# Splitting projection weights on ScalarE and VectorE, and weighting the token's own share of the shift while reading PSUM

## The chip, the cores and the metric

The kernel runs on one core of a Trainium2 chip. The metric is the device time of one execution in microseconds. The kernel before takes 4546.02 us (median of 3 runs, 4545.11 to 4547.92). The engines are named as in the profile: PE (TensorE matmul), PEld (its weight loads), DVE (VectorE), ACT (ScalarE), POOL (GpSimd), SP (the queue that issues most DMAs).

## The reference, cut to what matters

Two layers of a hybrid trunk over 2048 latent tokens and 256 context tokens, width 1024. Each layer normalises, projects into 32 blocks of 128 columns, mixes in three head groups, and projects back. The change touches only the input projection and the shift over tokens that follows it for the RWKV columns:

```python
def centred_shift(p, mu_prev, mu_next):
    prev = jnp.pad(p, ((0, 0), (1, 0), (0, 0)))[:, :-1]
    nxt = jnp.pad(p, ((0, 0), (0, 1), (0, 0)))[:, 1:]
    return p + mu_prev * (prev - p) + mu_next * (nxt - p)

    h = rms_norm(x, norm_w[l]) * (1.0 + scale) + shift
    ...
    pa, pb, pt = _split(h @ w_in[l], (RWKV_COLS, HGRN_COLS, ATTN_COLS))
    ...
    pa = centred_shift(pa.astype(F32), mu_prev, mu_next)
    r, k, v, wd_f, wd_b, ad_f, ad_b, g = _split(pa, RWKV_SPLITS)
```

The first 14 of the 32 blocks (`pa`) are shifted. The kernel computes the shift as (1 - mu_prev - mu_next) p + mu_prev prev + mu_next next; the first of these three weights is `mu0` in its code.

## The kernel before, in words

**Stages.** Each layer has an input projection (`inproj_phase`) and then a mixing phase (`phase2`: the RWKV and HGRN recurrences, the attention, the readout and the output projection). In the profile the input projection of the first layer runs from the start to about 1190 us, that of the second from about 2310 to 3495 us; the mixing phases fill the rest.

**The projection.** Activations lie in SBUF with features on partitions and tokens along the free dimension, as a rounded part and a remainder (`hi`, `lo`). The weights of one 128-column block arrive as 128 x 1024 float32 (`wraw`, one buffer, loaded from the POOL queue, L304) and are split in the same way by `split` (L307): `whi` is the rounded copy (L312) and `wlo` the remainder (the tensor_tensor of L313, which the trace records at the helper's line, L74). Each of the two has two buffers, so the split of block n+1 waits until PE is through with block n-1. `prefetch(n+1)` splits the next block and starts the load of the one after it; that load waits until the split has read `wraw`. A product is 24 matmuls into a PSUM tile `ps` (three buffers): whi and wlo against h's rounded part, and whi against its remainder.

**Two sweeps.** The tokens are done in two sweeps: 1280 tokens (as groups of 512, 256 and 512), then 1024 (two groups of 512). In each sweep the blocks follow one another in the list `order`: 32 in the first layer and 33 in the second, so there are 130 splits in all.

**After a group** (`group`, L339). ACT copies `ps` into `s` (two buffers) for unshifted blocks, and into `pb` (one buffer, with a column more on each side) for shifted ones. In the second layer the blocks in `free` leave out the context tokens.

**After a block** (`end`, L379). For a shifted block, DVE makes `s` from `pb`, for each segment of tokens: a tensor_scalar with mu0 (L392, recorded as L79) and two scalar_tensor_tensor that add the two neighbours (L393 and L394, recorded as L83). Then `post` runs what the block needs and stores it. After it, `behind` lets the preparation of the RWKV recurrence (`RwkvPrep`) advance: from the block at position 9 on, its matmuls (tiles `aps`, `apm`), its DVE work (`tk`, `th`, `lkk`, and the row-by-row inverses `Gs` and `inv`, 60 dependent instructions for one window) and its round trips to memory (`scr_Lx`, `scr_Dx`, `daT`) lie between the projection's matmuls on the same engines.

**Order.** Every engine executes its instructions strictly in the order of its own stream. That order is made at build time by a planner that simulates the engines, puts an instruction in when its inputs are ready in that simulation, and prefers what the program wrote earlier. At run time each instruction waits for its semaphores, and what stands behind it on its engine waits with it.

Beside the splits, POOL does the remainders of the activations for three quarters of each normalised block (`h`, L74), the edges of `pb` (L373, L375, L376, L385), and the load of `wraw`.

Of the kernel before, what the change touches and what calls it, by code (L numbers as in the profile page):

```python
# [9 lines left out]
F32 = mybir.dt.float32  # L10
# [3 lines left out]
AF = mybir.ActivationFunctionType  # L14
ALU = mybir.AluOpType
# [27 lines left out]
def W(ap, n):  # L43
    return ap[:, n:n + 1]


class Trunk:
# [227 lines left out]
    def inproj_phase(self, l, src, prep, start):  # L275
        nc, io, S = self.nc, self.io, self.scr
# [6 lines left out]
        with ExitStack() as ph:  # L283
# [23 lines left out]
            def split(n):  # L307
                if n < len(seq):
                    w = raw.pop(n)
                    hi = wsp.tile([128, KD, 128], F32R, name="whi", tag="whi")  # L310
                    lo = wsp.tile([128, KD, 128], F32R, name="wlo", tag="wlo")
                    nc.gpsimd.tensor_copy(hi, w)  # L312
                    self.tt(lo, w, hi.bitcast(F32), ALU.subtract, nc.gpsimd)  # L313
                    spl[n] = (hi, lo)

            def prefetch(n):
                if n in raw:
                    split(n)
                    load(n + 1)
# [19 lines left out]
            def group(sw, n, st, t0, bn, every):  # L339

                j, s, pb, skip, shifted = st
                hi, lo = spl[n]
                base = 1280 * sw
                c0, c1 = BLK if skip and t0 == 0 else 0, BLK + 2 if shifted and t0 == 0 else BLK
                if c0 >= c1:
                    return
                ps = self.pin.tile([128, 512], F32, name="ps", tag="ps")
                if bn > BLK:
                    c1 = bn
                hh, hl = h[t0]  # L350
                i = 0
                for k, wt, ht in [(k, wt, hh) for k in range(KD) for wt in (hi, lo)] + [(k, hi, hl) for k in range(KD)]:
                    self.mm(ps[:, c0:c1], wt[:, k, :], ht[:, k, c0:c1], i == 0, i == 23)
                    i += 1
                    if i % every == 0 and work:
                        next(work[0], None)
                if not shifted:
                    self.evac(l, j, s[:, t0 - base:t0 - base + bn], ps[:, 0:bn], t0 - base, bn)
                else:
                    o = t0 - base + (1 if t0 == 0 or sw else 2)  # L360
                    if c0 == 0:
                        self.act(pb[:, o:o + bn], ps[:, 0:bn], AF.Identity)
                    if t0 == 0:
                        self.act(pb[:, 1282:1283], ps[:, BLK:BLK + 1], AF.Identity)

# [13 lines left out]
            def end(sw, n, st):  # L379
                j, s, pb, skip, shifted = st  # L380
                spl.pop(n, None)
                base = 1280 * sw
                if shifted:
                    if sw == 0:
                        edge.tensor_copy(keep[:, j], pb[:, 1281:1282])  # L385
                        segs = [(256, 1024, 258)] + ([] if skip else [(0, 256, 1)])
                    else:
                        segs = [(1280, 1024, 1)]
                    m0, mp, mn = W(self.mu0[l], j), W(self.P(l, "mup"), j), W(self.P(l, "mun"), j)
                    for t0, bn, c in segs:  # L390
                        sv = s[:, t0 - base:t0 - base + bn]
                        self.ts(sv, pb[:, c:c + bn], m0, ALU.mult)  # L392
                        self.stt(sv, pb[:, c - 1:c - 1 + bn], mp, sv, ALU.mult, ALU.add)  # L393
                        self.stt(sv, pb[:, c + 1:c + 1 + bn], mn, sv, ALU.mult, ALU.add)  # L394
                blks = sorted(SWEEP[sw])
                if skip:
                    blks = [b for b in blks if b[0] > 0]
                self.post(l, j, s, base, blks)
# [19 lines left out]
            for sw in range(2):  # L418
                for pos in [0] + list(range(2, end_ + 1)):
                    n = len(order) * sw + pos  # L420
                    pair = range(2 if pos in (0, end_) else 1)
                    prefetch(n + 1)
                    sts = [begin(sw, order[pos + e]) for e in pair]
                    for gi, g in enumerate(SWEEP[sw]):
                        while any(a not in done for a in cut(g)):
                            next(work[0], None)
                        for e in pair:
                            group(sw, n + e, sts[e], g[0], g[1], 4 if n == 0 and gi == 0 else 6)
                            if g is SWEEP[sw][-1]:
                                if len(pair) == 2 and e == 0:  # L430
                                    spl.pop(n)
                                    prefetch(n + 2)
                                end(sw, n + e, sts[e])
                                behind(sw, pos + e)
                        if sw == 0 and pos == end_ and gi == 0:

                            work[0] = norm(cuts[1][:2], cuts[1][2:])
                    if sw == 0 and pos == end_:
                        while cuts[1][1] not in done:
                            next(work[0], None)  # L440
                        for _ in work[0]:
                            pass
                        work[0] = norm(cuts[1][2:])
                    if sw == 0 and pos == end_ - 2:
                        for a in cuts[1][:2]:
                            xn[a] = self.normed(l, src, a, BLK)
# [1204 lines left out]
```

## Time and profile before

| | |
|---|---|
| median of 3 runs | 4546.02 us |
| the profiled execution | 4540.61 us, its span 4538.8 us |
| granted clock of PE over the span | 0.929 of full speed |
| PE busy | 3941.3 us (87%) |
| DVE busy | 3164.2 us (70%) |
| ACT busy | 1984.9 us (44%) |
| POOL busy | 1390.9 us (31%) |
| POOL, rounded weights, 130 casts | 151.6 us |
| POOL, weight remainders, 130 subtractions | 335.3 us |
| DVE, own share of the shift, 78 products | 62.1 us |

Busy time is time in which an engine executes; issuing of DMAs and waiting for semaphores is not in it. The clock of PE has two levels, 2.4 GHz (1.0 in the profile) and 1.2 GHz (0.5); a mean of 0.92 over a stretch says that 16% of it ran at the lower one. Where a line of the trace has "idle before", it is the time in which the engine had nothing to execute just before, and the name behind the arrow is what ended it.

### The profile page before, as it was taken

Reading aid. Unit: us, or ns where it says so; the run is one execution under the profiler, and the core shown is the slowest. Engines: PE = TensorE matmul, PEld = TensorE weight load, DVE = VectorE, ACT = ScalarE, POOL = GpSimd, SP = SyncE. Lnnn points to the kernel's source line nnn. Section 1 sums busy time; section 2 is a strip of 40 time slices with the busy share of each in tenths; the row PEclk is TensorE's granted clock in tenths of the full one; section 3 lists DMA queues with packets and bytes.
Section 4 is the critical chain, followed back from the end, with each engine's and each line's share of the span. In section 5 each row is a group of like instructions: output and inputs, shape, how many; then the busy total and the mean of one; then the engine's idle time right before and its main releaser. Section 6 shows DMA issues by size and latency. Waiting matters only on the chain. (4 is left out here: it accounts for less than half of the span.)

```text
span 4538.8 us, 98552 instructions
## 1 busy us (share of the span) xinstructions
PE 3941.3 (87%) x39424; PEld 3217.7 (71%) x39424; DVE 3164.2 (70%) x5646; ACT 1984.9 (44%) x4050; POOL 1390.9 (31%) x1298
## 2 busy tenths in 40 slices
PE   7998898889789889868979988898887888988788
PEld 4767776777677777766758767776676777777676
DVE  3547777678577887777744777556775877777786
ACT  3414343443355555533424353333433555555443
POOL 2322233223233332242243212243222422333232
PEclk8999898999899999988989989899898999999899
DMA  5466654666643334346634476435665543334554
GB/s 202 144 200 197 198 158 121 190 197 190 167 123 107 106 105 115 91 118 214 209 117 129 143 231 195 116 106 172 197 185 159 135 113 101 97 104 126 171 187 132
DMA packets 777312, 688.41 MB, mean 152 GB/s; under 512 B 352164, under 2 KB 675044, under 8 KB 776856
## 3 DMA queue, kind: packets, MB, share of 16 engines
q1 hardware_dynamic: 747624, 583.93, 43.4%
q0 software_dynamic: 18720, 68.17, 5.2%
q10 hardware_dynamic: 10512, 30.02, 2.0%
q8 instruction: 312, 5.11, 0.5%
q14 instruction: 144, 1.18, 0.1%
HBM read 440.70 MB, written 241.22 MB: 150 GB/s over the span
## 5 line engine op out<-in xcount | busy, mean ns | idle before, releaser
L67 PE MATMUL ps<-h,whi 128*128 128x512 f32 x4160 | 1374.7, 406 | 18.2 <-ACT s L64 11.2
L67 PEld LDWEIGHTS ps<-h,whi 128*128 128x128 f32 x4160 | 806.0, 195 | 207.7 <-issue 19.5
L67 PE MATMUL ps<-h,wlo 128*128 128x512 f32 x2080 | 850.9, 409 | 5.2 <-POOL wlo L74 5.2
L312 POOL CAST whi<-wraw 128x1024 fp32r<-128x1024 f32 x130 | 151.6, 1166 | 1124.0 <-PE ps L67 991.8
L67 PEld LDWEIGHTS ps<-h,wlo 128*128 128x128 f32 x2080 | 411.7, 198 | 95.4 <-POOL wlo L74 6.3
L74 POOL TENSOR_TENSOR hE<-hb 128x256 f32<-128x256 f32 x408 | 290.9, 735 | 326.7 <-PE wps L67 195.7
L74 POOL TENSOR_TENSOR wlo<-wraw,whi 128x1024 fp32r<-128x1024 f32 x130 | 335.3, 2579 | 10.5
L1085 DVE COPY_PREDICATED hatt<-lm,wps 64x256 f32<-64x256 int32 x476 | 266.7, 560 | 29.8 <-PE wps L67 23.2
L64 ACT ACT_TABLE_LOAD x177 | 227.1, 1283 | 109.9 <-DVE s L79 33.4
L74 DVE TENSOR_TENSOR Gs<-can,inv 128x30 f32<-128x30 f32 (+9 forms) x540 | 238.9, 442 | 35.0 <-PE apm L67 23.7
L67 PE MATMUL pq<-KZ,BKs 128*64 128x128 f32 x2496 | 228.2, 297 | 34.9 <-DMA KZ<-scr_RK 18.8
L67 PE MATMUL opo<-wohi,ohi 128*128 128x512 f32 x544 | 216.2, 413 | 31.2 <-DVE og L74 18.6
L74 DVE TENSOR_TENSOR hQz<-hE,hqz 128x512 f32<-128x512 f32 x204 | 179.8, 882 | 76.4 <-DMA hqz<-scr_hq 67.8
L74 DVE TENSOR_TENSOR inv<-inv,Gs 128x30 f32<-128x30 f32 (+9 forms) x540 | 223.5, 414 | 12.1
L83 DVE SCALAR_TENSOR_TENSOR s<-pb,par,s 128x1024 f32<-128x1024 f32 (+1 forms) x156 | 217.3, 1393 | 5.6
L67 PE MATMUL opo<-wolo,ohi 128*128 128x512 f32 x544 | 212.9, 407 | 0.0
L64 ACT ACTIVATE pt<-wps 128x512 f32<-128x512 f32 (+1 forms) x288 | 149.4, 525 | 137.1 <-PE wps L71 132.7
L67 PEld LDWEIGHTS pq<-KZ,BKs 128*64 128x64 f32 x2496 | 169.4, 147 | 53.6 <-issue 19.8
L64 ACT ACTIVATE s<-ps 128x512 f32<-128x512 f32 (+1 forms) x175 | 95.8, 562 | 251.6 <-PE ps L67 222.8
L64 ACT ACTIVATE pb<-ps 128x512 f32<-128x512 f32 (+2 forms) x162 | 77.1, 492 | 290.5 <-PE ps L67 204.1
L71 PE MATMUL wps<-ident,prob 128*128 128x128 f32 x960 | 168.7, 292 | 40.8 <-DVE hatt L1085 22.8
L79 DVE TENSOR_SCALAR s<-pb,mu 128x1024 f32<-128x1024 f32 (+1 forms) x78 | 62.1, 796 | 194.7 <-ACT pb L64 193.9
(272 smaller groups left out, 9225.8 us busy)
## 6 DMA issues: line engine op xcount, KB each, us to landing
wraw<-in_w_in_dram POOLq DMA_DIRECT2D x128, 512.0 KB, 4.6
scr_KB<-tk SPq DMA_DIRECT2D x36, 768.0 KB
BKs<-scr_KB SPq DMA_DIRECT2D x144, 192.0 KB
KZ<-scr_RK SPq DMA_DIRECT2D x272, 96.0 KB
x<-in_mod_w_dram SPq DMA_DIRECT2D x32, 512.0 KB
lkk<-scr_kk SPq DMA_DIRECT2D x36, 384.0 KB
th<-scr_wa SPq DMA_DIRECT2D x36, 384.0 KB
scr_RK<-lkk SPq DMA_DIRECT2D x36, 384.0 KB
```

The source lines that it names most:

```text
L64: return self.nc.scalar.activation(out=out, in_=in_, func=func, **kw)
L67: return self.nc.tensor.matmul(out=out, lhsT=lhsT, rhs=rhs, start=start, stop=stop)
L71: return self.nc.tensor.transpose(out, in_, self.ident[0:p, 0:p])
L74: return (eng or self.nc.vector).tensor_tensor(out=out, in0=a, in1=b, op=op)
L79: return e.tensor_scalar(out=out, in0=a, scalar1=s1, scalar2=None, op0=op0)
L83: return (eng or self.nc.vector).scalar_tensor_tensor(out=out, in0=a, scalar=s, in1=b, op0=op0, op1=op1)
L312: nc.gpsimd.tensor_copy(hi, w)
L1085: nc.vector.copy_predicated(o, m, d)
```

## The change

`split` makes the rounded copy with an ACT activation (Identity) and the remainder with a DVE tensor_tensor, where POOL did both. In `group`, ACT reads each shifted product a second time from PSUM and writes it, multiplied by mu0, to `s`; in `end` DVE's multiplication by mu0 is gone, and its two additions stay.

```diff
@@ split
-                    nc.gpsimd.tensor_copy(hi, w)
-                    self.tt(lo, w, hi.bitcast(F32), ALU.subtract, nc.gpsimd)
+                    self.act(hi, w, AF.Identity)
+                    self.tt(lo, w, hi.bitcast(F32), ALU.subtract)
@@ group
                     if c0 == 0:
                         self.act(pb[:, o:o + bn], ps[:, 0:bn], AF.Identity)
+                        self.act(s[:, t0 - base:t0 - base + bn], ps[:, 0:bn], AF.Identity, scale=W(self.mu0[l], j))
@@ end
-                    m0, mp, mn = W(self.mu0[l], j), W(self.P(l, "mup"), j), W(self.P(l, "mun"), j)
+                    mp, mn = W(self.P(l, "mup"), j), W(self.P(l, "mun"), j)
                     for t0, bn, c in segs:
                         sv = s[:, t0 - base:t0 - base + bn]
-                        self.ts(sv, pb[:, c:c + bn], m0, ALU.mult)
                         self.stt(sv, pb[:, c - 1:c - 1 + bn], mp, sv, ALU.mult, ALU.add)
```

## Rows read from the trace of the kernel before

**Rows 1.** Stretches of the input projections: engines' busy us (instructions), clock, DMA share, GB/s.
```profile
60.00:350.00 290.00, 282.60 (x1369) 207.15 (x1368) 136.98 (x176) 102.50 (x164) 82.15 (x79) 0.98 0.54 169
350.00:1190.00 840.00, 741.62 (x5466) 613.60 (x5464) 625.72 (x1118) 343.10 (x545) 245.70 (x197) 0.92 0.59 177
2390.00:2550.00 160.00, 154.79 (x805) 130.15 (x803) 82.23 (x96) 65.19 (x101) 47.19 (x47) 0.95 0.41 124
2550.00:3495.00 945.00, 819.98 (x5855) 662.25 (x5854) 642.12 (x1144) 367.53 (x571) 265.13 (x217) 0.91 0.56 167
```
**Rows 2.** PE's waits, 350 to 1190 us: total us, times, longest us.
```profile
PE apm L67 <- DMA daT<-scr_Dx: 25.3, 13, 4.2
PE aps L67 <- DVE tk L699: 15.6, 7, 4.0
PE aps L67 <- DVE tk L74: 15.4, 6, 5.1
PE ps L67 <- POOL wlo L74: 2.0, 1, 2.0
```
**Rows 3.** PE's waits, 2550 to 3495 us.
```profile
PE apm L67 <- DMA daT<-scr_Dx: 37.7, 21, 8.1
PE aps L67 <- DVE tk L74: 18.5, 5, 9.8
PE ps L67 <- ACT s L64: 11.2, 3, 7.3
PE aps L67 <- DVE tk L699: 10.0, 6, 2.2
```
**Rows 4.** Costliest groups: busy us, mean ns | idle before, releasers.
```profile
L312 POOL CAST whi<-wraw 128x1024 fp32r<-128x1024 f32 x130 | 151.6, 1166 | 1124.0 <-PE ps L67 991.8
L74 POOL TENSOR_TENSOR wlo<-wraw,whi 128x1024 fp32r<-128x1024 f32 x130 | 335.3, 2579 | 10.5
L79 DVE TENSOR_SCALAR s<-pb,mu 128x1024 f32<-128x1024 f32 (+1 forms) x78 | 62.1, 796 | 194.7 <-ACT pb L64 193.9
```
**Rows 5.** POOL's timeline at 494 us: start us, us, instruction.
```profile
494.19 2.40 POOL L74 TENSOR_TENSOR wlo<-wraw,whi 128x1024 fp32r<-128x1024 f32 x1
```
**Rows 6.** DVE's timeline at 494 us.
```profile
494.34 2.47 DVE L74 TENSOR_TENSOR Gs<-can,inv 128x198 f32<-128x198 f32 x1
496.84 0.37 DVE L74 TENSOR_TENSOR inv<-inv,Gs 128x198 f32<-128x198 f32 x1
```
**Rows 7.** DVE's timeline, first and last instruction of the count.
```profile
115.82 3.09 DVE L83 SCALAR_TENSOR_TENSOR s<-pb,par,s 128x256 f32<-128x256 f32 x2
...
3459.08 2.42 DVE L74 TENSOR_TENSOR Gs<-can,inv 128x150 f32<-128x150 f32 x1
```
**Rows 8.** PE's timeline: first, one and last wait of the count.
```profile
146.37 1.13 PE L67 MATMUL pa<-t,bones 128*128 128x512 f32 x2 [0.32 <-ACT t L64]
...
504.61 1.65 PE L67 MATMUL aps<-lkk,tk 64*64 64x64 f32 x26 [5.06 <-DVE tk L74]
...
3373.26 2.04 PE L67 MATMUL aps<-lkk,tk 64*64 64x64 f32 x47 [4.32 <-DVE tk L74]
```
**Rows 9.** DVE, one group by shape: busy us, mean ns | idle before.
```profile
L83 DVE SCALAR_TENSOR_TENSOR s<-pb,par,s 128x1024 f32<-128x1024 f32 x112 | 193.2, 1725 | 4.5
```
**Rows 10.** Tile `s`: duration ns min/median/max, first and last start us, forms.
```profile
L83 DVE SCALAR_TENSOR_TENSOR s<-pb,par,s x156: 457/1277/3417, 115.8 to 3429.3; 128x1024 f32<-128x1024 f32 x112, 128x256 f32<-128x256 f32 x44
```
**Rows 11.** Tile `pb`: duration ns min/median/max, first and last start us, forms.
```profile
L74 DVE TENSOR_TENSOR s<-s,pb x8: 1224/1357/1493, 326.1 to 973.4; 128x1280 f32<-128x1280 f32 x4, 128x1024 f32<-128x1024 f32 x4
```
**Rows 12.** ACT groups by shape: busy us, mean ns | idle before, releasers.
```profile
L64 ACT ACTIVATE s<-ps 128x512 f32<-128x512 f32 x148 | 86.8, 595 | 224.3 <-PE ps L67 195.5 <-DMA scr_aq<-s 12.3 <-DMA scr_sgr<-s 8.1
L64 ACT ACTIVATE th<-aps,half 128x256 f32<-128x256 f32 x108 | 43.3, 472 | 85.3 <-PE aps L67 78.9 <-DVE Gs L74 5.3 <-DMA scr_Dx<-can 0.8
L64 ACT ACTIVATE t<-s,par 128x512 f32<-128x512 f32 x24 | 17.1, 713 | 42.5 <-DVE s L83 42.5
L64 ACT ACTIVATE wohi<-wo 128x1024 fp32r<-128x1024 f32 x16 | 16.8, 1052 | 21.1 <-DMA wo<-in_w_out_dram 21.0
```

## The prediction

> **What bounds the kernel now.** The change lies in the two input projections, so I read them first, by stretch (from 60 and 2390 us on, when the projection's matmuls run). In the 2235 us of [rows 1] PE is busy 283 + 742 + 155 + 820 = 1999 us: it is the engine that sets the end, and it idles 236 us. Its clock adds a second loss: the granted 0.98, 0.92, 0.95 and 0.91 leave 6 + 67 + 8 + 85 = 166 us of full speed unused, so each idle microsecond goes with 0.70 us lost at the lower level. DVE is busy 1487 us there (67%), ACT 878 us (39%). Nearly all of the loss is in the stretches from 350 and 2550 us, in which the RWKV preparation shares the engines; the two before them idle 13 us.
>
> Then PE's waits in those two stretches [rows 2, 3]. It waits for DVE's `tk` (L699 and L74: 59.5 us) and for `daT` (63 us), whose round trip starts when DVE and ACT are through with an inverse. It waits for a split only 2.0 us in the first stretch. So POOL's 487 us of splitting [rows 4] are hidden as far as their own completion goes, and making them shorter is worth nothing by itself.
>
> The third view is the timelines of POOL and DVE beside each other, and it shows what the splits do cost. At 494.19 POOL starts a remainder and takes 2.40 us [rows 5]; at 494.34 DVE starts a product of 128x198, which lasts 2.47 us, and the next instruction, of the same shape, 0.37 us [rows 6]. The two end together. DVE was held until POOL was done, and ten microseconds later PE waits 5.06 us for DVE's `tk` [rows 8]. After 60 us I counted 106 DVE instructions of the projections that overlap a split and run over 1 us longer than the 20th percentile of their own kind; [rows 7] has the first and the last of them. Their excess is 211 us; with the smaller ones it is 267 us. The lowest estimate that rows give alone: the 112 long additions of the shift average 1725 ns [rows 9] where the median of all is 1277 [rows 10], 112 x 0.448 = 50 us in this one group.
>
> The Trainium skill has a rule for this (SBUF — State Buffer, "Who interferes with whom"): VectorE and GpSimd share one pair of ports, a VectorE instruction with two SBUF inputs contends with a GpSimd instruction that reads SBUF, and the second one is blocked until the first is through. The 494 us rows agree. If every one of the 130 remainders blocked DVE for its whole mean, the held time would be 335 us and the forecast below would come out near 4467 us by the same steps; the counted 211 us decide.
>
> **The change part by part.**
>
> *Taken from DVE.* The 78 products with mu0, 62 us [rows 4], and the held time, of which I take 211 us (ends 50 and 267). Together 273 us.
>
> *Added to DVE.* 130 subtractions of 128x1024 with two SBUF inputs. The nearest rows are the 128x1024 and 128x1280 subtractions and minima on `s`, 1224 ns at least and 1493 at most [rows 11]: 130 x 1.224 = 159 us, which I take because the minimum is that of the 1024 shape; 194 us at the other end. So DVE's net relief is 273 - 159 = 114 us, 0.42 of what goes (0.29 with 194 us added, 0.52 with 267 us held; with 50 us held it would be a loss of 47 us).
>
> *What PE gains from it.* Of 117 waits of PE over 0.3 us in these stretches, 58 come within 8 us after a DVE instruction that was held by over 1 us in all ([rows 8]: the first, one, and the last). Each can shrink at most by the held time before it: 85 us in all, as the upper limit of what the removal alone could give. Since the subtractions return part of the load to DVE's stream, I take the same 0.42 of it: 36 us (25 to 44). With 0.70 us of clock for each of them, 25 us more (0 to 31).
>
> *Added to ACT.* 130 casts at 1.052 us, the same shape and conversion as `wohi` [rows 12]: 137 us. 112 scaled reads of 512 and 22 of 256 columns. No row has this form: an unscaled read of 512 takes 0.595 us, an activation of 512 with a scale from a parameter tile 0.713, one of 256 with a bias tile 0.472 [rows 12]. I take 0.65 and 0.47, 83 us (75 to 90). ACT goes from 878 to about 1098 us, 49% of the stretches. Three PSUM buffers of 24 matmuls each cover a late read; PE waited 11.2 us for ACT's `s` in the second projection [rows 3], and a quarter more load makes that 3 us more.
>
> *Moved earlier: the claim on `s`.* A shifted block now writes `s` at its first group, not after its last. The buffer must be free of block n-2: its DVE work and its stores. If it isn't, ACT stands, and behind it the reads of later groups and the preparation's exponentials. Today's 148 unshifted reads lose 12.3 + 8.1 us of ACT's time to such stores [rows 12]; as much for 112 more is 15 us, and PE sees a third, 5 us. With the 3 us above, ACT's side costs 8 us (0 to 20).
>
> *New waits.* The rounded copy waits for the last matmul of block n-1, as it does on POOL, which stood there 992 us in all [rows 4]. On ACT the read of that same block's last group waits for the same matmul and stands ahead, so this wait adds nothing as long as that order holds. On DVE the subtraction waits for ACT's copy, with inverse steps and shift additions queued behind it; the shift additions wait for ACT's last read anyway. POOL's next load of `wraw` now waits for DVE; behind it are only remainders of `h` and edges of `pb`, which stood behind POOL's splits before. I cost these at nothing; the cover is one block's 48 or 72 matmuls, which lie between a split and its use. If it goes, the price is in the last rival.
>
> *POOL.* 487 us fewer, worth nothing beyond the above.
>
> *The sum.* 4540.6 - 36 - 25 + 8 = 4487.6 us against the profiled execution. The median shown is 5.4 us above that one, so I forecast 4493 us.
>
> **The rivals.**
>
> *More than that.* All 85 us go, because the planner, which ordered DVE's stream without the held time, now finds the engines where it expects them, and the clock gains 60 us: 4546 - 145 + 8 = 4409 us. For it: the inverse is a chain of 60 dependent instructions, and one hold delays all behind it. Against it: 159 us of new work in the same stream.
>
> *No gain.* The work is only moved: DVE's own 159 us stand where the held time stood, and PE's waits are those at the end of a round trip to memory; 4546 us. For it: 63 us of waits for `daT` [rows 2, 3]. Against it: 211 us held exceed the 159 us. The Trainium skill says as much of moving work between VectorE and GpSimd (Perfetto Trace Analysis, "Optimizing Scalar/DVE Operations"): because of the shared port it "might not help". The held time in this trace bears out the port, and for that very reason not the conclusion.
>
> *Slower.* The subtraction comes late, because it now stands in DVE's stream, and the next block's matmuls with `wlo` wait. The place is the preparation's stretches, where DVE is 75% and 68% busy [rows 1] and has been late by up to 9.8 us [rows 3]. A late DVE result costs PE 33.9 / 11 = 3.1 us [rows 2, 3], with the clock 5.2 us. Ten late splits undo the forecast's 53 us; 13 of the 130 give +68, 4561 us. Against it: a split has a whole block's matmuls of time, and in the kernel before PE waited for only one split in the first stretch [rows 2].
>
> **How the numbers follow.** The forecast has 0.58 and a range of its own from 4470 to 4525; more than that 0.12, no gain 0.13, slower 0.17. The range that should hold the time reaches halfway to the larger gain and past the slower case: 4435 to 4565 us. A measurement of this kernel tells 0.2%, 9 us, from no change. Faster: 0.58 + 0.12 + 0.02 of the no-gain case = 0.72; the same 0.10; slower 0.18.
>
> **What would show it.** Right: the shift's long additions at about 1.27 us on average; DVE busy about 110 us less in the four stretches, ACT about 220 us more; PE's idle time there near 200 us and its clock a few hundredths higher; no PE wait on `wlo` of note. Wrong: DVE instructions still held, by POOL's other work; PE waiting for DVE's `wlo` or for ACT's `s`; idle time of PE unchanged with DVE lighter, which would mean that the waits I counted were not made by the held time.

## The result, and the profile after

The changed kernel takes 4407.77 us (median of 4 runs, 4394.95 to 4410.3) against 4546.97 us before: a ratio of 0.968, 95% interval 0.966 to 0.970 (as recorded; the two medians alone give 0.969). That is 139 us less, 2.6 times the forecast's 53 us, and outside its range (4435 to 4565). The rival "more than that" had priced 4409 us, with a chance of 0.12. The two profiled executions, from which the figures below come, lie 130 us apart.

The page of the changed kernel, busy time by engine:

```profile
span 4408.5 us, 98655 instructions
PE 3907.5 (89%) x39424; PEld 3188.1 (72%) x39424; DVE 2993.5 (68%) x5698; ACT 2173.6 (49%) x4308; POOL 893.3 (20%) x1038
```

DVE is 171 us less busy than before, ACT 189 us more, POOL 498 us less. To see where the time went, I cut each run into its two input projections (from the first matmul of `ps` to the last one, in each layer) and the rest; "the projections" below means this cut. The stretches of the kernel before in this cut (columns: length, then busy time of PE, PEld, DVE, ACT, POOL with the instructions, clock, DMA share, GB/s):

```profile
48.30:1184.00 1135.70, 1033.91 (x6850) 827.90 (x6850) 764.29 (x1293) 446.63 (x711) 330.10 (x275) 0.93 0.57 173
2336.40:3493.60 1157.20, 1015.70 (x6822) 820.80 (x6822) 746.80 (x1287) 449.59 (x705) 336.19 (x282) 0.91 0.53 158
```

and of the changed kernel:

```profile
49.40:1108.30 1058.90, 1005.26 (x6756) 801.38 (x6757) 667.58 (x1278) 534.82 (x835) 91.13 (x150) 0.96 0.61 184
2276.10:3366.20 1090.10, 1002.74 (x6638) 811.57 (x6637) 668.85 (x1317) 546.41 (x833) 87.69 (x152) 0.93 0.56 166
```

The two projections take 2149 us where they took 2293: 144 us less, and the rest of the span is 14 us longer. PE idles 141 us in them where it idled 243 (length less busy time), and is busy 42 us less; its clock rises from 0.93 and 0.91 to 0.96 and 0.93. DVE is 175 us less busy.

This cut leaves a part of the RWKV preparation out. After the last `ps` matmul of a layer the preparation still has work, and the next phase already runs beside it. Of the preparation's 3456 `apm` matmuls 192 came behind the cut before, and 470 do now; in the first layer the last of them ends 41 us after the last `ps` matmul before, 59 us now. So I also cut each layer at whichever ends later, the last `ps` or the last `apm` matmul, and call that the input stage. The first layer before (the second has the same line as above), then both layers of the changed kernel:

```profile
48.30:1225.30 1177.00, 1062.00 (x7338) 852.35 (x7340) 787.32 (x1343) 462.73 (x740) 336.85 (x284) 0.92 0.58 173
49.40:1167.70 1118.30, 1044.63 (x7600) 835.72 (x7602) 706.17 (x1373) 557.61 (x882) 97.70 (x160) 0.95 0.61 184
2276.10:3369.90 1093.80, 1005.85 (x6826) 814.53 (x6824) 669.92 (x1319) 548.13 (x836) 87.69 (x152) 0.93 0.56 167
```

The input stage takes 2212 us where it took 2334: 122 us less, with PE idle 162 us instead of 256, and what follows it is 8 us shorter. By either cut the gain lies where the change is.

What answers to [rows 4], [rows 9] and [rows 12], by line and shape (busy us, mean ns | idle before, releasers):

```profile
L74 DVE TENSOR_TENSOR wlo<-wraw,whi 128x1024 fp32r<-128x1024 f32 x130 | 158.4, 1218 | 95.9 <-ACT whi L64 95.8
L64 ACT ACTIVATE whi<-wraw 128x1024 fp32r<-128x1024 f32 x130 | 137.5, 1058 | 49.9 <-DMA wraw<-in_w_in_dram 46.1 <-PE ps L67 3.7
L64 ACT ACTIVATE s<-ps,mu 128x512 f32<-128x512 f32 x134 | 86.8, 650 | 31.1 <-DMA scr_r<-s 10.5 <-DMA scr_wa<-s 9.6 <-DMA scr_hq<-s 3.8
L83 DVE SCALAR_TENSOR_TENSOR s<-pb,par,s 128x1024 f32<-128x1024 f32 x112 | 143.3, 1279 | 115.2 <-ACT s L64 110.7 <-issue 4.3
```

The prices of the new instructions were right: subtractions 158 us (forecast 159), casts and scaled reads 137 + 87 = 224 us (220). The last line is the one to look at: the same 112 additions take 1279 ns on average where they took 1725 [rows 9]. Their instruction is the same; what stood beside them is gone. That is 50 us in this group, the prediction's lowest estimate. DVE's timeline now has the subtraction among its neighbours, and each takes its own time (start us, us, instruction):

```profile
497.41 0.68 DVE L74 TENSOR_TENSOR s<-s,t 128x512 f32<-128x512 f32 x1
498.01 1.22 DVE L74 TENSOR_TENSOR wlo<-wraw,whi 128x1024 fp32r<-128x1024 f32 x1
499.15 0.35 DVE L74 TENSOR_TENSOR Gs<-can,inv 128x198 f32<-128x198 f32 x1
```

The product of 128x198 that took 2.47 us in [rows 6] takes 0.35 us here. PE's waits in the first projection, 350 to 1150 us (total us, times, longest):

```profile
PE aps L67 <- DVE tk L699: 12.3, 8, 2.3
PE apm L67 <- DMA daT<-scr_Dx: 11.8, 11, 2.3
...
PE ps L67 <- ACT whi L64: 3.3, 3, 1.8
...
PE aps L67 <- DVE tk L74: 1.8, 3, 0.8
```

and in the second, 2450 to 3370 us:

```profile
PE apm L67 <- DMA daT<-scr_Dx: 30.4, 14, 5.4
PE ps L67 <- ACT s L64: 16.6, 4, 7.6
...
PE aps L67 <- DVE tk L699: 7.2, 5, 2.7
...
PE ps L67 <- DVE wlo L74: 0.5, 1, 0.5
```

Against [rows 2, 3], the waits for `tk` (L74) fall from 33.9 to 2.1 us (0.3 of them in the second stretch, not shown), those for `daT` from 63 to 42 us, those for `tk` (L699) from 26 to 20. The waits for ACT's `s` grow from 11 to 17 us. For the splits PE waits 6 us in both stretches together, with 2.0 us that are not shown.

### The profile page after: what moved, and what is told of

Same layout as the page of the kernel before. It is cut to its first block, busy times and chain, and to the rows that moved or that the text cites. A ratio compares the mean times of both kernels' runs of the same rounds, so it can differ in the third digit from the quotient of the medians.

```text
span 4408.5 us, 98655 instructions
## 1 busy us (share of the span) xinstructions
PE 3907.5 (89%) x39424; PEld 3188.1 (72%) x39424; DVE 2993.5 (68%) x5698; ACT 2173.6 (49%) x4308; POOL 893.3 (20%) x1038
## 5 line engine op out<-in xcount | busy, mean ns | idle before, releaser
L304 POOL DMA_DIRECT2D wraw<-in_w_in_dram x128 | 69.2, 540 | 1669.9 <-DVE wlo L74 1382.3
L74 POOL TENSOR_TENSOR hE<-hb 128x256 f32<-128x256 f32 x408 | 291.3, 736 | 327.9 <-PE wps L67 195.8
L83 DVE SCALAR_TENSOR_TENSOR s<-pb,par,s 128x1024 f32<-128x1024 f32 (+1 forms) x156 | 164.3, 1054 | 182.8 <-ACT s L64 128.4
L74 DVE TENSOR_TENSOR hQz<-hE,hqz 128x512 f32<-128x512 f32 x204 | 185.8, 911 | 89.9 <-DMA hqz<-scr_hq 86.8
L74 DVE TENSOR_TENSOR wlo<-wraw,whi 128x1024 fp32r<-128x1024 f32 x130 | 158.4, 1218 | 95.9 <-ACT whi L64 95.8
L67 PE MATMUL wps<-hQz,hE 128*64 128x64 f32 (+1 forms) x2992 | 149.8, 239 | 56.2 <-DVE hatt L1085 30.8
L74 DVE TENSOR_TENSOR Gs<-can,inv 128x30 f32<-128x30 f32 (+9 forms) x540 | 182.7, 338 | 18.5 <-PE apm L67 7.5
L64 ACT ACTIVATE hE<-hE 128x512 f32<-128x512 f32 x204 | 128.4, 631 | 131.1 <-POOL hE L74 121.6
```

Source lines behind the costliest of these rows:

```text
L64: return self.nc.scalar.activation(out=out, in_=in_, func=func, **kw)
L67: return self.nc.tensor.matmul(out=out, lhsT=lhsT, rhs=rhs, start=start, stop=stop)
L74: return (eng or self.nc.vector).tensor_tensor(out=out, in0=a, in1=b, op=op)
L83: return (eng or self.nc.vector).scalar_tensor_tensor(out=out, in0=a, scalar=s, in1=b, op0=op0, op1=op1)
L304: (nc.sync, nc.scalar, nc.gpsimd)[CFG["wq"]].dma_start(out=w, in_=io["vw1"][l - 1] if j == 32 else io["w_in"][l, j])
```

## The experiments

Theory H says that POOL's reads hold DVE and that this held time was the cost. Theory L says that DVE's total own work is what counts, theory P that the planner happened upon a better order. All ratios are against the kernel before on the same chip and carry a 95% interval. "Held time" is worked out from each trace as in the prediction: over all DVE instructions of the projections that overlap a given POOL work, the time above the 20th percentile of their own kind. For the kernel before, with all instructions counted, it is 219 us beside the remainders and 43 us beside the casts, 262 us together (most of the 43 us is in instructions that lie beside a cast and a remainder); for the changed kernel there is no such work, and 13 us remain beside POOL's remainders of `h`.

**The split alone.** The kernel before with

```diff
-                    nc.gpsimd.tensor_copy(hi, w)
-                    self.tt(lo, w, hi.bitcast(F32), ALU.subtract, nc.gpsimd)
+                    self.act(hi, w, AF.Identity)
+                    self.tt(lo, w, hi.bitcast(F32), ALU.subtract)
```

> The kernel before with the splits on ACT and DVE; the product with mu0 stays on DVE. Theory H (held time: a POOL remainder blocks DVE's two-input instructions, and PE waits for what stands behind them): the split alone carries the gain, 4405 to 4425 us. Theory L (DVE's load: what counts is DVE's total busy time, whoever causes it): the 62 us of products are a third of DVE's net relief of 170 us, so a third of the gain is missing, about 4455 us. Theory P (the planner happened upon a better order): any time between 4400 and 4550 us.

4429.05 us, ratio 0.972 (0.969 to 0.974). The projections (same columns):

```profile
49.10:1110.50 1061.40, 995.14 (x6754) 794.01 (x6754) 692.79 (x1319) 498.78 (x766) 92.11 (x150) 0.97 0.61 184
2289.70:3365.10 1075.40, 991.27 (x6632) 804.69 (x6630) 691.25 (x1353) 505.04 (x765) 86.66 (x152) 0.93 0.56 168
```

They take 2137 us, 12 less than with mu0 on ACT, though DVE is 48 us busier; the input stage takes 2223 us, 11 more. So the split carries nearly all of the gain. The 0.35% by which the total is behind the changed kernel is about what another order makes by itself (below), so these runs don't tell whether mu0 adds anything. The median lies 4 us above H's range; the kernel before takes 4555 us on this chip, 8 us more than in the first comparison.

**The shift weight alone.** The changed kernel with the split put back:

```diff
-                    self.act(hi, w, AF.Identity)
-                    self.tt(lo, w, hi.bitcast(F32), ALU.subtract)
+                    nc.gpsimd.tensor_copy(hi, w)
+                    self.tt(lo, w, hi.bitcast(F32), ALU.subtract, nc.gpsimd)
```

> The changed kernel with both halves of the split back on POOL; ACT still applies mu0 as it reads PSUM. H: the held time is back, 4520 to 4550 us. L: DVE is 62 us lighter than in the kernel before, a third of the gain, about 4500 us. P: any time between 4400 and 4550 us.

4563.45 us, ratio 1.001 (0.999 to 1.003): no gain. The held time is 260 us, as before, and the projections take 2305 us. 46 us less of DVE busy time in them bought nothing, which speaks against L. The time is 13 us above H's range.

**The cast on ACT, the remainder on POOL.** The changed kernel with

```diff
-                    self.tt(lo, w, hi.bitcast(F32), ALU.subtract)
+                    self.tt(lo, w, hi.bitcast(F32), ALU.subtract, nc.gpsimd)
```

> The changed kernel with only the remainder back on POOL: ACT casts, POOL subtracts. The remainder reads two SBUF tiles for 2.4 us each time, so H: the held time of some 210 us is back and the time is 4510 to 4550 us, though DVE has 159 us of subtractions less than in the changed kernel. A rival that prices only DVE's own instructions expects less than the changed kernel's 4408 us. P: any time between 4400 and 4550 us.

4515.77 us, ratio 0.990 (0.988 to 0.993). The held time beside the remainders is 212 us, and the same additions of the shift show it (by shape, columns as above):

```profile
L83 DVE SCALAR_TENSOR_TENSOR s<-pb,par,s 128x1024 f32<-128x1024 f32 x112 | 205.4, 1834 | 127.0 <-ACT s L64 118.6 <-issue 6.0
```

```profile
50.10:1177.50 1127.40, 1022.69 (x6850) 819.58 (x6850) 724.58 (x1266) 541.12 (x842) 254.39 (x213) 0.94 0.57 174
2331.50:3461.10 1129.60, 1011.88 (x6822) 820.59 (x6820) 696.45 (x1250) 544.38 (x833) 253.46 (x217) 0.92 0.54 161
```

DVE has 130 subtractions fewer than in the changed kernel and is 85 us busier all the same; the projections are 108 us longer. A count of DVE's own instructions has the sign wrong here.

**The cast on POOL, the remainder on DVE.** The changed kernel with

```diff
-                    self.act(hi, w, AF.Identity)
+                    nc.gpsimd.tensor_copy(hi, w)
```

> The changed kernel with only the cast back on POOL: POOL casts in 1.04 us each, DVE subtracts. In the kernel before, DVE instructions beside a cast alone exceeded their kind by 12 us in all. H: 4410 to 4430 us, a little held time by the casts. If ACT's new load (137 us of casts) had cost something, up to 20 us less than the changed kernel, 4390 to 4408. P: any time between 4400 and 4550 us.

4460.07 us, ratio 0.979 (0.976 to 0.981); the expected 4410 to 4430 was too little. The casts hold DVE 51 us, four times what I had read for them (I had counted only instructions that overlapped a cast and nothing else). The projections take 2165 us, 16 more than the changed kernel's, and the input stage 2256 us, 44 more: nearly all of the 1.1% lies there, because the preparation ends later. How much of it is held time, and how much the subtraction's wait for POOL's cast, no run separates.

**POOL reads again.** The changed kernel, with a subtraction of the weights from themselves behind each load; its result goes to a small tile that nothing reads:

```diff
                     split(n)
                     load(n + 1)
+                    hi = spl[n][0].bitcast(F32).rearrange("p k c -> p (k c)")
+                    wdm = wsp.tile([128, 256], BF16, name="wdm", tag="wdm", bufs=1)
+                    for e in range(0, 1024, 256):
+                        self.tt(wdm, hi[:, e:e + 256], hi[:, e:e + 256], ALU.subtract, nc.gpsimd)
```

> The changed kernel, and after each split and the next load POOL subtracts the rounded weights from themselves in four pieces of 256 columns into a small tile that nothing reads (some 0.65 us each, 2.6 us per split, two SBUF inputs). Nothing waits for it, DVE and ACT have exactly the changed kernel's instructions. H: each piece holds DVE up to its own length, the held time is near 200 us again and the two projections grow by some 100 to 140 us: 0.99 to 1.00 of the kernel before. L (DVE's own instructions): as the changed kernel, 0.968. P: any ratio between 0.965 and 1.00, and then the kernel with memsets in its place as far from the changed kernel as this one.

**POOL writes only.** The control, with

```diff
+                    wdm = wsp.tile([128, 256], BF16, name="wdm", tag="wdm", bufs=1)
+                    for e in range(12):
+                        nc.gpsimd.memset(wdm, 0.0)
```

> The control for the run before it: POOL is busy at the same places with 12 memsets of the small tile, which write SBUF and read nothing. H: no held time by them, the time stays within 1% of the changed kernel, 0.965 to 0.978 of the kernel before. If POOL being busy, the load of the next weights behind it, or the new order made the difference, this run is as slow as the one with reads.

With reads 4510.02 us, ratio 0.989 (0.986 to 0.993); with writes 4441.51 us, ratio 0.975 (0.972 to 0.978). POOL's work, the shift's additions, the projections and the input stage in the run with reads:

```profile
L74 POOL TENSOR_TENSOR wdm<-whi 128x256 bf16<-128x256 f32 x520 | 504.8, 971 | 1217.7 <-ACT whi L64 1195.1
L83 DVE SCALAR_TENSOR_TENSOR s<-pb,par,s 128x1024 f32<-128x1024 f32 x112 | 159.0, 1420 | 130.2 <-ACT s L64 121.3 <-DMA lkk<-scr_kk 5.0 <-issue 3.8
50.70:1170.70 1120.00, 1024.30 (x6758) 814.08 (x6760) 740.33 (x1277) 541.31 (x840) 326.90 (x398) 0.94 0.57 174
2357.00:3463.40 1106.40, 1004.72 (x6632) 813.30 (x6632) 737.99 (x1318) 537.82 (x829) 335.86 (x414) 0.92 0.54 164
50.70:1236.60 1185.90, 1070.05 (x7600) 854.33 (x7602) 780.01 (x1373) 564.04 (x885) 333.96 (x408) 0.93 0.57 173
2357.00:3481.70 1124.70, 1011.74 (x6849) 819.65 (x6849) 740.98 (x1322) 545.22 (x837) 336.91 (x415) 0.92 0.55 164
```

and in the run with writes:

```profile
L322 POOL MEMSET wdm<- 128x256 bf16 x1560 | 499.6, 320 | 83.0
L83 DVE SCALAR_TENSOR_TENSOR s<-pb,par,s 128x1024 f32<-128x1024 f32 x112 | 143.3, 1280 | 123.5 <-ACT s L64 116.4 <-issue 5.0 <-POOL wdm L322 2.0
53.50:1128.50 1075.00, 1000.39 (x6758) 801.76 (x6756) 668.01 (x1279) 540.84 (x838) 298.82 (x805) 0.96 0.60 181
2296.10:3378.90 1082.80, 1002.60 (x6638) 813.32 (x6638) 671.67 (x1317) 549.63 (x835) 342.11 (x934) 0.93 0.56 167
53.50:1191.40 1137.90, 1040.78 (x7604) 837.49 (x7602) 707.43 (x1375) 564.26 (x885) 306.03 (x815) 0.95 0.60 181
2296.10:3387.90 1091.80, 1009.18 (x6848) 819.36 (x6846) 672.90 (x1319) 551.34 (x838) 342.64 (x936) 0.92 0.56 168
```

POOL is busy with them for 500 us in both, and DVE has the same instructions. They stand at the same place of the program, but the reads wait for ACT's `whi` and the memsets for nothing, so they don't fall at the same moments. With reads DVE is 142 us busier than in the changed kernel, the projections are 77 us longer and the input stage 98; with writes 3 us busier, 9 and 18 us longer. No wait of ACT, DVE or PE is put down to the reads themselves. So it is the reading. The Trainium skill's rule (SBUF — State Buffer, "Who interferes with whom": VectorE instructions with two SBUF inputs contend with a GpSimd instruction that reads SBUF, not with one that only writes it) agrees with both runs. The total lies at 0.989, just below what H expected, and the projections' 77 us are less than its 100 to 140; the four short pieces held some 142 us and not 200.

**DVE's work doubled.** The changed kernel with

```diff
                     self.tt(lo, w, hi.bitcast(F32), ALU.subtract)
+                    self.tt(lo, w, hi.bitcast(F32), ALU.subtract)
```

> The changed kernel with each weight remainder computed twice by DVE, 158 us more of DVE's own work in the projections. The forecast's step that priced DVE's relief as a net load (0.42 of the held time's effect, because 159 us of subtractions come in) says that this undoes the relief: the time goes back to 0.99 to 1.00 of the kernel before. H: what the subtractions cost where they stand is small, as PE has a whole block of matmuls before it needs them: 0.970 to 0.980.

4462.11 us, ratio 0.979 (0.977 to 0.981). DVE's 130 further subtractions make it 126 us busier in the projections, and these 17 us longer. The projections, then the input stage:

```profile
49.10:1136.80 1087.70, 1013.80 (x6658) 809.10 (x6658) 725.60 (x1319) 536.78 (x835) 104.66 (x151) 0.95 0.58 178
2317.20:3395.50 1078.30, 988.20 (x6632) 799.78 (x6630) 737.29 (x1363) 544.75 (x831) 100.46 (x151) 0.94 0.55 168
49.10:1222.00 1172.90, 1071.58 (x7730) 859.87 (x7730) 771.95 (x1438) 568.99 (x895) 111.11 (x160) 0.93 0.58 176
2317.20:3426.50 1109.30, 1006.35 (x6944) 814.37 (x6944) 751.08 (x1393) 557.72 (x854) 104.71 (x157) 0.93 0.56 169
```

The netting of the forecast expected 0.99 to 1.00; the doubling took back a third of the gain (0.011 of 0.032), not all of it. But it was not nearly free either. In the projections a microsecond of DVE's own work costs 0.13 us, against 77 / 142 = 0.54 us for a held one; only, part of the preparation was put off. 576 `apm` matmuls come behind the last `ps` matmul, where the changed kernel has 470, and the input stage is 70 us longer, 0.48 us for each of its 147 us more of DVE. PE waits 12.0 us in 8 waits for `wlo`, in the changed kernel 1.6 us in 4.

**The split first, once and twice.** The changed kernel with a priority in the planner. The second run, shown here, also has the doubled subtraction; the first has it once:

```diff
-                    self.act(hi, w, AF.Identity)
-                    self.tt(lo, w, hi.bitcast(F32), ALU.subtract)
+                    with self.tc.high_priority(offset=300):
+                        self.act(hi, w, AF.Identity)
+                        for _ in range(2):
+                            self.tt(lo, w, hi.bitcast(F32), ALU.subtract)
```

> The changed kernel with a higher priority for both halves of the split in the planner (offset 300), so that ACT and DVE do them as soon as the buffers are free, ahead of the preparation. It is the control for the next run. 0.965 to 0.980 if it matters little where the subtraction stands.

> The run before with the remainder computed twice: 158 us more of DVE's own work, known to the planner, at the very place where POOL's remainder used to hold DVE. If a hold costs so much because of when it falls (right behind the release of the weights, ahead of the shift and the preparation), this costs 0.5 us per us, 80 us more than the run before in the projections. If it costs so much because the planner did not count with it, this costs like the doubled subtraction without priority, 17 us or so.

Once 4464.41 us, ratio 0.980 (0.978 to 0.983); twice 4485.62 us, 0.985 (0.983 to 0.988). The projections and then the input stage, first with the subtraction once, then twice:

```profile
50.60:1144.40 1093.80, 1013.39 (x6850) 806.12 (x6850) 669.10 (x1288) 540.11 (x842) 92.60 (x151) 0.95 0.59 179
2320.90:3403.10 1082.20, 997.48 (x6632) 808.75 (x6630) 668.44 (x1317) 552.80 (x837) 93.97 (x152) 0.93 0.55 167
50.60:1199.80 1149.20, 1049.13 (x7516) 837.05 (x7518) 703.68 (x1369) 560.67 (x883) 99.37 (x160) 0.94 0.59 178
2320.90:3416.60 1095.70, 1005.17 (x6848) 815.66 (x6846) 669.51 (x1319) 556.32 (x841) 93.97 (x152) 0.92 0.56 167
```

```profile
49.10:1129.60 1080.50, 1004.86 (x6658) 800.09 (x6658) 730.15 (x1314) 533.15 (x833) 105.40 (x150) 0.96 0.59 179
2326.30:3421.50 1095.20, 999.86 (x6632) 808.26 (x6630) 736.80 (x1360) 547.38 (x833) 106.61 (x151) 0.93 0.55 166
49.10:1217.90 1168.80, 1064.05 (x7786) 852.20 (x7788) 780.18 (x1441) 565.40 (x893) 112.57 (x160) 0.94 0.59 177
2326.30:3455.30 1129.00, 1019.76 (x6984) 824.06 (x6982) 752.70 (x1395) 561.31 (x858) 110.98 (x157) 0.92 0.56 166
```

The projections take 2176 us in both, 27 more than the changed kernel's, from the priority or the new order that comes with it. At the place where POOL's remainder used to fall, 129 us more of DVE busy time cost the projections nothing, but again work was put off: 576 `apm` matmuls behind them instead of 384, and the input stage is 53 us longer. The whole loses 0.005, some 22 us. The two readings that the run was to tell apart, 80 us and 17 us, both miss, and the question stays open. That held time costs more because the planner does not know of it is an inference: no run shows a plan that knows of the holds.

**Another order.** The changed kernel with one memset of two columns on POOL per load:

```diff
+                    nc.gpsimd.memset(wsp.tile([128, 2], F32, name="wdm", tag="wdm", bufs=1), 0.0)
```

> The changed kernel with one memset of two columns on POOL after each load of weights: 0.1 us of work that nothing waits for, but the planner builds another order from it (thousands of places differ on each engine). It measures the scatter that a new order brings by itself: H expects the projections within 20 us of the changed kernel's 2149 us and the whole between 0.965 and 0.978. P: it may lose most of the gain.

4418.21 us, ratio 0.971 (0.968 to 0.974), projections 1058.3 + 1075.5 = 2134 us. This new order moves the projections by 15 us and the total by 0.3%, and leaves the input stage at 2212 us; it does not lose the gain. P fails, and differences of that size between the runs above mean nothing. It is one draw: what follows the input stage takes between 2182 and 2232 us in the runs so far, though their edits have no instruction there.

The runs that price held time and DVE's own work, side by side (us more than the run it is compared with; the last column is the difference of the two unrounded ratios times 4555 us):

| run | compared with | DVE busy, input stage | projections | input stage | whole |
|---|---|---|---|---|---|
| POOL reads | changed kernel | 145 | 77 | 98 | 97 |
| POOL reads | POOL writes | 141 | 69 | 81 | 66 |
| subtraction twice | changed kernel | 147 | 17 | 70 | 50 |
| split first, twice | split first, once | 160 | 0 | 53 | 22 |
| other order | changed kernel | 4 | -15 | 0 | 13 |

By the whole time a held microsecond costs 0.47 to 0.67 us and one of DVE's own 0.14 to 0.34; by the input stage 0.58 to 0.68 and 0.33 to 0.48. The other order's 13 us would be 0.09 in such a price. Held time is the dearer, by less than the projections alone make it look.

**Further work off POOL.** The changed kernel with the remainders of the activations on DVE (the planner's setting `nl` from 2 to 8), and with four kinds of POOL work of the mixing phases on DVE (each loses its `nc.gpsimd`):

> The changed kernel with all remainders of the normalised activations on DVE (54 subtractions that POOL did in 1.29 us each while DVE lost 13 us beside them). H: 0 to 13 us less than the changed kernel, 0.965 to 0.969. If POOL's latency on these was on PE's path, more than that. L: DVE gets some 35 us more of its own, up to 25 us slower.

> The changed kernel with four kinds of POOL work of the mixing phases on DVE: the remainders of the output weights (16), of the readout (17), the difference before the HGRN exponential (36), the residual add (68). DVE instructions beside them exceed their kind by 24 + 24 + 17 + 39 = 104 us in the changed kernel; on DVE they would take some 20 + 16 + 25 + 47 = 108 us. If a held microsecond costs PE 0.55 us and one of DVE's own 0.11, as the runs so far have it in the projections, the gain is 57 - 12 = 45 us against the changed kernel, 0.958 of the kernel before. If in the mixing phases DVE is simply the fuller engine (80% busy), the two cancel: 0.967 to 0.975.

The first gives 4432.26 us, 0.973 (0.971 to 0.975), projections 2157 us: no gain from 13 us of held time, within the scatter of orders in the projections, and in total outside the expected 0.965 to 0.969. The second gives 4396.37 us, 0.965 (0.963 to 0.968): the lowest time of all runs, but its interval overlaps the changed kernel's, the expected 0.958 is outside it, and of the other reading's 0.967 to 0.975 only the end touches it. In the mixing phases removing some 104 us of holds for 108 us of own work gained some 12 us by the ratios, where the prices of the projections gave 45; another order alone makes 13, so whether it gained anything these runs don't tell.

## Why the prediction was wrong

- **The mechanism was right.** POOL's remainders held DVE, and PE waited for what stood behind. The runs with reads and with writes show it, and the split alone carries nearly all of the gain.
- **The step that failed is PE's gain, 85 us x 0.42 = 36 us of idle time.** PE's idle time fell by 102 us in the projections, 95 us in the input stage. Both factors were too low.
- **The 0.42.** "Since the subtractions return part of the load to DVE's stream, I take the same 0.42 of it": held time and DVE's own work were added up as one load of one price. They aren't: doubling the subtractions, 147 us more of DVE, cost the whole 50 us, the 145 us that POOL's reads added to DVE 97 us. By that step the doubling should have undone the gain, and it took back a third.
- **The cap of 85 us.** The idle time fell by more than the whole of it, with 159 us of new work in DVE's stream. It counted only what was held within 8 us ahead of a wait. The same count done again on the trace gives 80 us with 8 us and some 150 with 20 (a longer stretch also takes in chance neighbours), so the cap hung on that choice. It also rested on the 211 us in instructions held by over 1 us; all held time was 262 us, and DVE became 175 us less busy where the forecast had 114. The 0.54 of the run with reads gives 262 x 0.54 = 142 us, close to the projections' 144, but that leaves out DVE's new work, so the agreement is no proof.
- **The clock.** The projections are shorter by the 102 us of idle time and 42 us of busy time. Over the whole span the same 39424 matmuls keep PE busy 34 us less. That answers to the clock: `ps` matmuls of 512 columns take 389 ns at the higher level and 628 at the lower (medians) before and after alike, and 247 instead of 286 lie at the lower. It is 0.33 us for each idle microsecond, where the forecast took 0.70, a figure that counts the lower clock over idle time too. So the forecast's 25 us (36 x 0.70) came near the 34 by two errors.
- **ACT's side was right in size.** 224 us of new work, `s` claimed earlier with 31 us of waits before the scaled reads (15 expected), PE's wait for ACT's `s` up by 5 us in the second projection (8 allowed).
- **"New waits" at nothing held for the change.** The subtraction waits for ACT's copy (96 us of DVE idle time), POOL's load for the subtraction, and PE for a split 6 us in two stretches. The slower rival, a late subtraction, did not come about; with the subtraction doubled PE's waits for `wlo` reach 12 us.
- **The mu0 part** was netted with the rest as DVE load; by itself it gives nothing (1.001), and on top of the split no more than another order does.
- **The chances.** "More than that" had 0.12 and a range that stopped halfway to it. What spoke for it was in the rows: one hold delays all the dependent instructions behind it. What I set against it, 159 us of new work in the same stream, cost less than the same time held. That its 4409 us were met to 1 us is in part luck: it had 85 us of idle time and 60 us of clock, and 102 and 42 were measured in the projections.

## What to carry to other kernels

Where a two-input instruction of DVE takes several times what its neighbours of the same shape take, look at POOL's timeline for an instruction that reads SBUF and ends with it: that time is in DVE's busy time. Don't net it one for one against work that you move to DVE: here a held microsecond cost the whole 0.47 to 0.67 us, one of DVE's own work 0.14 to 0.34. These prices are of this stage; in the mixing phases the same exchange gained no more than a new order. Where the order is planned anew with every edit, measure an edit without meaning too (here 0.3% of the whole), and compare the stage that was changed before the total. Cut that stage where its last work ends: to the last matmul of the projection the doubled subtraction cost 17 us, to the end of the preparation 70 and in the whole 50, because the work that it put off fell behind the first cut.

## What the runs showed of the hardware that I had not expected

- POOL's casts, with one SBUF input, also held DVE: 43 us before, 51 us in the run where they were alone on POOL, for 130 casts of 1.04 us (median).
- POOL is held in turn: its 520 dummy subtractions of 256 columns average 971 ns where their median is 757 and their least 602. The longest took 7.09 us and lies beside an unbroken row of DVE instructions with two inputs, which began 0.14 us before it and took their usual times, such as 1.22 us for the subtraction:

```profile
2705.39 7.09 POOL L74 TENSOR_TENSOR wdm<-whi 128x256 bf16<-128x256 f32 x1 [18.43 <-ACT whi L64]
2705.25 0.38 DVE L74 TENSOR_TENSOR inv<-inv,Gs 128x210 f32<-128x210 f32 x1
2705.54 1.22 DVE L74 TENSOR_TENSOR wlo<-wraw,whi 128x1024 fp32r<-128x1024 f32 x1
```

- 1560 memsets on POOL, as long in all as those reads, left the shift's additions at 1280 ns, the changed kernel's 1279.
